# Output weights split early through DRAM, a start tile by tile, and smaller moves inside attention, in a two-layer streaming trunk

## The chip, the cores and the metric

The kernel runs on one core of a Trainium2 chip. The metric is the device time of one execution in microseconds, as the median of several runs. A core has five engines that run their own instruction queues side by side: TensorE (PE, matrix products and transposes; its weight loads are listed as PEld), VectorE (DVE), ScalarE (ACT), GpSimd (POOL) and SyncE (SP, which here issues transfers). Engines wait for each other through semaphores, and each works through its own queue in order.

## The reference

A two-layer trunk over 1024 positions of width 1024, in fp32. Each layer normalises its input, projects it once, runs three branches on slices of the projection, norms each branch, and adds the projected result:

```python
def hybrid_layer(x, positions, pre_g, w_in, ..., branch_g, w_out, post_g):
    h = rms_norm(x, pre_g)
    proj = h @ w_in
    xa, ga, q_lat, kv_lat, k_rope, gb, u, v, gc = jnp.split(proj, offsets, axis=-1)
    ya = rg_lru(causal_depthwise_conv(xa, conv_w, conv_b), wa, ba, wx, bx, lam) * jax.nn.silu(ga)
    yb = mla(q_lat, kv_lat, k_rope, positions, q_norm_g, w_uq, kv_norm_g, w_ukv) * jax.nn.silu(gb)
    yc = spatial_gating(u, v, sgu_g, sgu_bn, sgu_w, sgu_b) * jax.nn.silu(gc)
    y = jnp.concatenate([rms_norm(ya, ...), rms_norm(yb, ...), rms_norm(yc, ...)], axis=-1)
    return x + rms_norm(y @ w_out, post_g)
```

`mla` is attention with 6 heads (queries and keys of 96, values of 64) whose mask lets a position see its own chunk of 64 and all chunks before it. The branches have widths 384, 384 and 256.

## The kernel before

**Precision.** Every fp32 product is three products of a faster type (fp32r): a tensor is split into a high part, which ACT makes as a copy, and a low part, the difference, which DVE or POOL makes; `mm3` (line 124) multiplies high by high, high by low and low by high. Each weight tile and each activation that is multiplied therefore costs one ACT copy and one subtraction.

**Buffers.** Three pools of SBUF slots: `RS` (33 slots of 128x1024, for split parts), `FS` (7 fp32 slots, and rows of `Y` that are lent to it while they hold nothing) and `HS` (3 small scratch slots). `ring` holds small per-row numbers. In PSUM the banks are `pw` (two wide ones) and `pa` (four).

**Stages of a layer.** `prenorm` (line 325) squares a tile on ACT, makes the factor on POOL (`rsqrt`, line 129) and scales the tile; `turn_pair` (line 331) transposes two normed tiles and splits them. `group` (line 553) makes the inputs and gates of the recurrent branch, two column blocks at a time; then come a stage for u and v, one token tile at a time (`toks`, line 397), a stage for gc, the latent projection (`C_LAT`), the gate of attention (`C_GB`), and attention. Attention goes through 24 units of (head, pair of 128-row tiles). Each unit has `scores` (line 882: products, maximum on DVE, exponential with its sum on ACT, reciprocal on DVE, scaling on POOL) and `mixv` (line 926: transposes of the probabilities, their split, products with the values, and the gated sum of the two halves into `Y`). Scores run two units ahead of `mixv`, queries four. `project` (line 967) multiplies `Y` by `w_out` for one token tile: the first five of eight row blocks, then the last three, whose scale comes from the statistics of the attention branch (`stats`, line 510). After `project` a tile is normed, added to the input, stored, and normed again for the next layer.

**`w_out`.** From unit 8 on, whenever enough slots are free, `load_wo` (line 986) loads one of the eight row blocks of 128x1024 and splits it right there: eight ACT copies per layer and eight low parts, three of them on DVE (`WO_ON_V`), five on POOL. All transfers of the kernel are issued by SP.

**The start.** `load_pre_gain` and two tiles of x are loaded, then the first weights (`W`, line 358, in two parts of four row blocks), two more tiles, four more, and the second weights. The first two tiles are normed as a pair, so that both factors are made by one operation, then the next two, and the four others are normed by POOL.

**What sets the order.** The program order is only a wish: a scheduler places each instruction by its own timeline, and `keep` pins an instruction to its place in program order. The engine of an operation is written in the code; `Q_ON_V`, `Y_ON_V` and `WO_ON_V` are lists of the cases that go to DVE instead of POOL.

## Time and profile before

| | |
|---|---|
| median of 3 runs | 930.64 us (930.25 to 930.79) |
| the profiled execution | 928.53 us, its span 926.6 us |
| mean granted clock of PE | 0.993 |
| busy: PE, weight loads | 880.2 us (95%), 776.2 us (84%) |
| busy: DVE, ACT, POOL | 581.8 us (63%), 514.6 us (56%), 384.9 us (42%) |
| moved by transfers | 53.37 MB, 58 GB/s over the span |
| second attention loop, first attention loop | about 695 to 860 us, 245 to 400 us |

Times in the rows are microseconds from the start of the span. A group of rows comes from one of three views. The *table of stretches* cuts the span into windows; its columns are the window, its length, the busy time and number of instructions of PE, PEld, DVE, ACT and POOL, the mean granted clock of PE (1.00 is full), the busy share of the transfer engines, and GB/s. A *timeline* lists instructions in order; its columns are start, duration, engine, line, operation, output<-inputs with their shapes and types, count, and in brackets the idle time of that engine just before with the name of what ended it. The *groups by shape* sum the instructions of one line and shape; after the bar stand the busy time, the mean duration in ns, and the idle time before them. `R`, `F`, `H` are slots of the three pools.

### The profile page before, as it was taken

To read this page: it belongs to the slowest core of one execution; us is meant where nothing else is said; L and a number is where in the kernel's file an instruction comes from. 1 tells how busy PE (TensorE), PEld (TensorE's weight loads), DVE (VectorE), ACT (ScalarE), POOL (GpSimd) and SP (SyncE) were. 2 spreads that over 40 slices of the span, in tenths; PEclk is the share of its full clock that TensorE was granted. 3 is DMA by queue.
4 is the path that set the end of the run, shared out by engine and by line. 5 is a ranking of instruction groups with operands and counts; after the bars stand their busy time and mean duration, and the time that the engine had idled before them with its cause. 6 is when DMAs were issued, how large, how long until landed. Compare 5 with 4: busy or idle time off the path is not lost. (4 is left out here: it accounts for less than half of the span.)

```text
span 926.6 us, 13545 instructions
## 1 busy us (share of the span) xinstructions
PE 880.2 (95%) x5078; PEld 776.2 (84%) x5078; DVE 581.8 (63%) x1088; ACT 514.6 (56%) x1026; POOL 384.9 (42%) x407
## 2 busy tenths in 40 slices
PE   4999999999999988989999999999999998899997
PEld 3998789998898877878898888899988997788786
DVE  4568966355589988344455588354647898853422
ACT  6447634346577877344553485334567777754312
POOL 4720024152156567365743000524403566655822
PEclk9999999999999999989999999999999999999999
DMA  7201400111000211022432042000200002201322
GB/s 274 55 25 56 120 24 1 42 46 27 1 1 24 80 57 48 23 91 91 138 115 76 1 129 69 24 18 24 49 1 1 23 25 68 69 25 47 120 107 91
DMA packets 35862, 53.37 MB, mean 58 GB/s; under 512 B 7800, under 2 KB 25812, under 8 KB 35796
## 3 DMA queue, kind: packets, MB, share of 16 engines
q1 hardware_dynamic: 35796, 52.50, 17.7%
q8 instruction: 40, 0.66, 0.3%
q14 instruction: 26, 0.21, 0.1%
HBM read 44.10 MB, written 8.39 MB: 57 GB/s over the span
## 5 line engine op out<-in xcount | busy, mean ns | idle before, releaser
L125 PE MATMUL pw<-R,R 128*128 128x512 f32 (+1 forms) x704 | 259.1, 369 | 4.6 <-ACT F L916 2.3
L127 PE MATMUL pw<-R,R 128*128 128x512 f32 (+1 forms) x704 | 252.8, 360 | 0.0
L126 PE MATMUL pw<-R,R 128*128 128x512 f32 (+1 forms) x704 | 252.0, 358 | 0.0
L125 PE MATMUL pa<-R,R 128*128 128x512 f32 (+3 forms) x540 | 187.5, 349 | 2.7 <-DVE R L346 1.6
L127 PE MATMUL pa<-R,R 128*128 128x512 f32 (+3 forms) x540 | 185.9, 345 | 0.0
L126 PE MATMUL pa<-R,R 128*128 128x512 f32 (+3 forms) x540 | 185.7, 344 | 0.0
L125 PEld LDWEIGHTS pw<-R,R 128*128 128x128 f32 x704 | 134.3, 191 | 25.5 <-ACT F L916 5.0
L127 PEld LDWEIGHTS pw<-R,R 128*128 128x128 f32 x704 | 133.9, 190 | 18.5 <-POOL R L375 0.4
L126 PEld LDWEIGHTS pw<-R,R 128*128 128x128 f32 x704 | 134.3, 191 | 17.4
L125 PEld LDWEIGHTS pa<-R,R 128*128 128x128 f32 x540 | 102.0, 189 | 13.9 <-DVE R L346 2.3
L375 POOL TENSOR_TENSOR R<-F,R 128x1024 fp32r<-128x1024 f32 (+1 forms) x22 | 50.3, 2300 | 145.4 <-ACT R L374 145.3
L127 PEld LDWEIGHTS pa<-R,R 128*128 128x128 f32 x540 | 101.9, 189 | 9.9
L126 PEld LDWEIGHTS pa<-R,R 128*128 128x128 f32 x540 | 102.2, 189 | 8.4
L918 POOL TENSOR_SCALAR F<-F,ring 128x128 f32<-128x128 f32 (+3 forms) x96 | 76.3, 799 | 68.4 <-DVE ring L917 65.8
L356 DVE TENSOR_TENSOR R<-pa,R 128x512 fp32r<-128x512 f32 (+1 forms) x120 | 74.2, 628 | 21.4 <-ACT R L355 20.5
L916 ACT ACTIVATE F<-pw,ring 128x128 f32<-128x128 f32 (+3 forms) x96 | 70.9, 740 | 26.0 <-DVE ring L914 21.4
L914 DVE TENSOR_REDUCE ring<-pw 128x1 f32<-128x128 f32 (+3 forms) x96 | 71.5, 748 | 14.5 <-PE pw L907 13.8
L355 ACT ACTIVATE R<-pa 128x512 fp32r<-128x512 f32 (+1 forms) x120 | 64.3, 552 | 23.8 <-PE pa L938 18.7
L947 PE MATMUL pa<-R,R 128*128 128x256 f32 x480 | 72.5, 288 | 4.3 <-DVE H L956 2.4
L938 PE MATMUL pa<-ident,F 128*128 128x128 f32 x432 | 66.1, 276 | 10.9 <-DVE R L356 6.3
L947 PEld LDWEIGHTS pa<-R,R 128*128 128x128 f32 x480 | 63.5, 189 | 7.8 <-DVE H L956 3.7
L938 PEld LDWEIGHTS pa<-ident,F 128*128 128x128 f32 x432 | 50.4, 141 | 17.2 <-POOL Y L959 2.8
(271 smaller groups left out, 1328.0 us busy)
## 6 DMA issues: line engine op xcount, KB each, us to landing
F<-in_w_in SPq DMA_DIRECT2D x24, 512.0 KB, 4.3
F<-in_w_out SPq DMA_DIRECT2D x16, 512.0 KB, 4.0
F<-in_x SPq DMA_DIRECT2D x13, 512.0 KB, 4.5
F<-x SPq DMA_DIRECT2D x8, 512.0 KB, 4.2
x<-F SPq DMA_DIRECT2D x7, 512.0 KB
out_y<-F SPq DMA_DIRECT2D x7, 512.0 KB
...
```

Of the source, the lines that this page charges most:

```text
L125: PE.matmul(ps, lhsT=sh, rhs=mh, start=start, stop=False)
L126: PE.matmul(ps, lhsT=sh, rhs=ml, start=False, stop=False)
L127: PE.matmul(ps, lhsT=sl, rhs=mh, start=False, stop=stop)
L355: S_.activation(h, src, AF.Copy)
L356: (eng or G).tensor_tensor(out=lo, in0=src, in1=h.bitcast(F32), op=ALU.subtract)
L375: self.eng.tensor_tensor(out=lo, in0=st, in1=h.bitcast(F32), op=ALU.subtract)
L914: V.tensor_reduce(out=mx, in_=sv, axis=AX.XY, op=ALU.max, negate=True)
L916: S_.activation(p[:, 0:n].rearrange("p (a b) -> p a b", a=sv.shape[1]), sv, AF.Exp, bias=mx, accum_out=sm)
L918: G.tensor_scalar(out=p[:, 0:n], in0=p[:, 0:n], scalar1=rs, scalar2=1.0, op0=ALU.mult, op1=ALU.mult)
L938: PE.transpose(pv[:, c, i * 128:(i + 1) * 128], p[i][:, b * 128:(b + 1) * 128], ident)
L947: PE.matmul(o, lhsT=sv, rhs=pt[:, part, c * 256:(c + 1) * 256], start=(b == 0 and part == 0), stop=(b == nb - 1 and part == 1))
```

## The change

It has five parts.

1. **`w_out` is split early and kept in DRAM.** A new function `stage_wo` loads one row block, splits it into two `FS` slots and stores both parts into `wo_dram`. It is called for seven blocks in the stage of u and v and for the eighth in the stage of gc. `load_wo` no longer splits; it loads the two ready parts, with transfers that POOL issues.
2. **The start goes tile by tile.** The loads of two x tiles stand first, before the pre-norm gains and the first weights. The first three or four tiles are normed singly. The low part of the first half of the first weights is made by DVE; their second half is split inside `turn_pair`, between transposes. The first half group is walked block by block over the two outputs, the group (1, 0) of the first layer stands before the transposes of tiles 4 to 7 and takes them in between, and those tiles are normed by DVE.
3. **The gated sum.** In the 13 units of `Y_ON_V` ACT copies both halves out of PSUM and POOL adds them; DVE only multiplies by the gate. The other units are as before.
4. **Reciprocals by pairs.** The two tiles of a unit share one reciprocal.
5. **Engines of some splits.** The split of `Y` in `project` is on DVE for token tiles 2 and 3. `Q_ON_V` keeps two of its four entries, `WO_ON_V` is gone.

```diff
-Q_ON_V = ((0, 0), (0, 1), (1, 1), (4, 0))
+Q_ON_V = ((0, 0), (0, 1))
...
-WO_ON_V = (1, 4, 5)
...
+    wo_dram = [[dram.tile([128, 1024], F32, name=f"wo{k}{c}") for c in "hl"] for k in range(8)]
...
-        def split(self, order=lambda i: i):
-            for st in self.staged:
+        def split(self, order=lambda i: i, eng=None, n=8):
+            now, self.staged = self.staged[:n], self.staged[n:]
+            for st in now:
...
-                self.eng.tensor_tensor(out=lo, in0=st, in1=h.bitcast(F32), op=ALU.subtract)
+                (eng or self.eng).tensor_tensor(out=lo, in0=st, in1=h.bitcast(F32), op=ALU.subtract)
...
+    xn = [load_x(A["x"][0], t) for t in range(2)]
     load_pre_gain()
-    xn = [load_x(A["x"][0], t) for t in range(2)]
-    ws = {0: W(0, 0, 256, 4)}
+    ws = {0: W(0, 0, 256, 4, now=False)}
     xn += [load_x(A["x"][0], t) for t in range(2, 4)]
     hT = [new_hT()]
+    ws[1] = W(0, 256, 256, 4, now=False)
     x4 = [load_x(A["x"][0], t) for t in range(4, NT)]
-    ws[1] = W(0, 256, 256, 4, now=False)
     prow = load_params()
-    prenorm(xn[:2], xn[:2])
-    turn_pair(0, xn[:2], hT, 0, FS)
-    prenorm(xn[2:], xn[2:])
+    for i in range(2):
+        prenorm(xn[i:i + 1], xn[i:i + 1])
+    ws[0].split(eng=V, n=1)
+    turn_pair(0, xn[:2], hT, 0, FS, {0: lambda: ws[0].split(keep), 1: lambda: prenorm(xn[2:3], xn[2:3], keep),
+                                     3: lambda: prenorm(xn[3:4], xn[3:4], keep)})
+    ws[1].split(keep)
+    turn_pair(0, xn[2:], hT, 1, FS)
     for p in range(2):
-        prenorm(x4[2 * p:2 * p + 2], x4[2 * p:2 * p + 2], keep, G)
-    turn_pair(0, xn[2:], hT, 1, FS)
-    ws[1].split(keep)
+        prenorm(x4[2 * p:2 * p + 2], x4[2 * p:2 * p + 2], keep)
...
+            group(1, 0, lambda m: turn_pair(l, xn[2 * m:2 * m + 2], hT, 2 + m, xs, order=keep))
...
+        def stage_wo(k):
+            r = W_ROWS[k]
+            st, hi = FS.take((128, 1024)), FS.take((128, 1024))
+            h, lo = hi.bitcast(F32R), st.bitcast(F32R)
+            nc.sync.dma_start(out=st, in_=A["w_out"][l, r:r + 128, :])
+            if k < 5:
+                S_.activation(h, st, AF.Copy)
+                G.tensor_tensor(out=lo, in0=st, in1=hi, op=ALU.subtract)
+            else:
+                g = bgain(r // 128)
+                S_.activation(h, st, AF.Copy, scale=g)
+                V.scalar_tensor_tensor(out=lo, in0=st, scalar=g, in1=hi, op0=ALU.mult, op1=ALU.subtract)
+            for t, d in zip((hi, st), wo_dram[k]):
+                nc.sync.dma_start(out=d, in_=t)
+            FS.give(st)
+            FS.give(hi)
...
+            if t:
+                stage_wo(t - 1)
...
+            if t == 1:
+                stage_wo(7)
...
+            V.reciprocal(out=rs, in_=sm)
+            for i, p in enumerate(res):
+                n = (2 * j + i + 1) * 128
+                G.tensor_scalar(out=p[:, 0:n], in0=p[:, 0:n], scalar1=rs[:, i:i + 1], scalar2=1.0, op0=ALU.mult,
+                                op1=ALU.mult)
...
-            tmp = HS.take((128, 256))
-            S_.activation(tmp[mine], o[other], AF.Copy, scale=0.5)
-            V.scalar_tensor_tensor(out=tmp[mine], in0=o[mine], scalar=0.5, in1=tmp[mine],
-                                   op0=ALU.mult, op1=ALU.add)
+            tmp = HS.take((128, 2, 256))
...
+            S_.activation(tmp[mine, 0], o[other], AF.Copy, scale=0.5)
+            if on_v:
+                S_.activation(tmp[mine, 1], o[mine], AF.Copy, scale=0.5)
+                G.tensor_tensor(out=tmp[mine, 0], in0=tmp[mine, 1], in1=tmp[mine, 0], op=ALU.add)
...
-            split(Y[:, a:b, ts], yh[:, a:b], yl[:, a:b], G)
+            split(Y[:, a:b, ts], yh[:, a:b], yl[:, a:b], V if t in (2, 3) else G)
...
+            parts = RS.take((128, 1024)), RS.take((128, 1024))
+            for t, d in zip(parts, wo_dram[len(wo)]):
+                G.dma_start(out=t, in_=d)
+            wo.append(parts)
```

How instructions stand on an engine, at three places. In these pieces a number behind a name tells buffers of one pool apart: `F_134` to `F_139` are x tiles, weights or probabilities in `FS`, `R_...` split parts in `RS`, `H_...` scratch, `pa_...` and `pw_...` PSUM banks.

DVE at the start, before: both tiles are scaled (L328), then four low parts of the transposed tiles (L346), then the next two tiles.

```order
L328 TENSOR_SCALAR F_134<-F_134,ring 128x1024
L328 TENSOR_SCALAR F_135<-F_135,ring 128x1024
L346 SCALAR_TENSOR_TENSOR R_106<-pa_66,pg,R_105 128x256
L346 SCALAR_TENSOR_TENSOR R_108<-pa_67,pg,R_107 128x256
L346 SCALAR_TENSOR_TENSOR R_110<-pa_68,pg,R_109 128x256
L346 SCALAR_TENSOR_TENSOR R_112<-pa_65,pg,R_111 128x256
L328 TENSOR_SCALAR F_138<-F_138,ring 128x1024
L328 TENSOR_SCALAR F_139<-F_139,ring 128x1024
```

DVE at the start, after: the two scalings stand apart with the copy of the gains between them, and the low part of the first weights (L378) and the clearing of a gate matrix (L419) stand ahead of the low parts of the tiles.

```order
L328 TENSOR_SCALAR F_134<-F_134,ring 128x1024
L190 COPY pg<-pa_65 128x16
L328 TENSOR_SCALAR F_135<-F_135,ring 128x1024
L378 TENSOR_TENSOR R_110<-F_136,R_109 128x1024
L419 MEMSET F_136 128x768
L346 SCALAR_TENSOR_TENSOR R_102<-pa_66,pg,R_101 128x256
L346 SCALAR_TENSOR_TENSOR R_104<-pa_67,pg,R_103 128x256
L346 SCALAR_TENSOR_TENSOR R_106<-pa_68,pg,R_105 128x256
```

The subtraction at L378 has moved here from POOL.

POOL in the first layer's attention, before: splits of `w_out` (L356), scalings of probabilities (L918) and gated products (L959) take turns.

```order
L959 TENSOR_TENSOR Y<-Y,H_143 64x256
L918 TENSOR_SCALAR F_137<-F_137,ring 128x768
L942 MEMSET R_111 128x2x128
L356 TENSOR_TENSOR R_122<-F_138,R_120 128x1024
L918 TENSOR_SCALAR F_140<-F_140,ring 128x896
L959 TENSOR_TENSOR Y<-Y,H_142 64x256
L918 TENSOR_SCALAR F_136<-F_136,ring 128x1024
L356 TENSOR_TENSOR R_115<-F_139,R_114 128x1024
```

POOL at the same place, after: the loads of the ready parts (L1030, `wo1h` is the high part of block 1) stand between scalings (L954, the former L918) and gated products (L1000, the former L959).

```order
L954 TENSOR_SCALAR F_137<-F_137,ring 128x384
L954 TENSOR_SCALAR F_137<-F_137,ring 128x512
L1000 TENSOR_TENSOR Y<-Y,H_142 64x256
L1030 DMA R_110<-wo1h 128x1024
L1030 DMA R_124<-wo1l 128x1024
L1030 DMA R_120<-wo2h 128x1024
L1030 DMA R_115<-wo3l 128x1024
L1030 DMA R_114<-wo3h 128x1024
L954 TENSOR_SCALAR F_134<-F_134,ring 128x640
L954 TENSOR_SCALAR F_139<-F_139,ring 128x768
L1030 DMA R_122<-wo2l 128x1024
L1000 TENSOR_TENSOR Y<-Y,H_141 64x256
```

The splits of `w_out` are gone from this queue and 16 issues of transfers per layer have come into it, five of them in a row here.

PE at the end of the first layer's attention, before: after the last product with values (L947) four matmuls of `project` stand ahead of the statistics of the attention branch (L522).

```order
L947 MATMUL pa_68<-R_110,R_118 128x256 x4
L125 MATMUL pw_63<-R_123,R_107 128x512
L126 MATMUL pw_63<-R_101,R_107 128x512
L125 MATMUL pw_64<-R_125,R_107 128x512
L126 MATMUL pw_64<-R_126,R_107 128x512
L522 MATMUL pa_66<-ones,H_142 128x1 x4
```

PE at the same place, after: L983 is the former L947, L124 to L126 are the three products of `mm3`, and L524 is the former L522; the rows left out are matmuls of `project` too, 40 in all from the last L983 to the L524.

```order
L983 MATMUL pa_68<-R_116,R_118 128x256 x4
L983 MATMUL pa_68<-R_106,R_118 128x256 x4
L124 MATMUL pw_63<-R_123,R_103 128x512
L125 MATMUL pw_63<-R_109,R_103 128x512
L124 MATMUL pw_64<-R_125,R_103 128x512
...
L126 MATMUL pw_64<-R_112,R_108 128x512
L124 MATMUL pw_64<-R_112,R_103 128x512
L524 MATMUL pa_66<-ones,H_141 128x1 x4
L125 MATMUL pw_64<-R_133,R_103 128x512
```

So 36 more matmuls of 512 columns stand between the attention products and the statistics.

## Rows read from the trace of the kernel before

**Rows 1.** Table of stretches; columns as told under the table before.
```profile
0.00:20.00 20.00, 6.46 (x25) 5.21 (x25) 8.33 (x15) 11.83 (x21) 8.52 (x15) 1.00 0.86 314
20.00:100.00 80.00, 79.96 (x463) 70.45 (x464) 56.34 (x121) 47.20 (x72) 22.70 (x12) 1.00 0.18 52
240.00:286.00 46.00, 45.70 (x287) 41.22 (x286) 39.73 (x90) 34.48 (x86) 19.84 (x31) 1.00 0.00 1
286.00:360.00 74.00, 64.61 (x435) 57.74 (x435) 68.30 (x125) 57.77 (x123) 49.23 (x55) 1.00 0.17 58
690.00:738.00 48.00, 47.37 (x285) 41.85 (x285) 38.41 (x86) 35.64 (x84) 18.25 (x29) 1.00 0.00 1
738.00:811.00 73.00, 65.93 (x434) 58.98 (x432) 63.50 (x124) 56.92 (x123) 47.57 (x55) 0.98 0.18 58
```

**Rows 2.** Timeline of ACT at the start; columns as told under the table before.
```profile
4.33 1.06 ACT L317 ACTIVATE H<-F 128x1024 bf16<-128x1024 f32 x1 [2.33 <-DMA F<-in_x]
...
8.02 1.06 ACT L317 ACTIVATE H<-F 128x1024 bf16<-128x1024 f32 x1 [2.54 <-DMA F<-in_x]
...
9.40 1.06 ACT L374 ACTIVATE R<-F 128x1024 fp32r<-128x1024 f32 x1 [0.24 <-DMA F<-in_w_in]
...
14.85 0.47 ACT L345 ACTIVATE R<-pa,pg 128x256 fp32r<-128x256 f32 x1 [1.47 <-PE pa L339]
```

**Rows 3.** Timelines of POOL, DVE and PE at the start, and one later DVE row.
```profile
9.57 0.73 POOL L134 TENSOR_TENSOR ring<-ring,mhalf 128x2 f32<-128x2 f32 x1
10.53 5.53 POOL L375 TENSOR_TENSOR R<-F,R 128x1024 fp32r<-128x1024 f32 x2 [0.23 <-ACT R L374]
...
10.33 3.51 DVE L328 TENSOR_SCALAR F<-F,ring 128x1024 f32<-128x1024 f32 x2 [5.06 <-POOL ring L134]
...
486.30 0.75 DVE L328 TENSOR_SCALAR Y<-F,ring 128x1024 f32<-128x1024 f32 x1 [1.31 <-POOL ring L134]
...
13.90 2.82 PE L339 MATMUL pa<-ident,F 128*128 128x128 f32 x12 [1.64 <-DVE F L328]
16.38 0.78 PE L125 MATMUL pw<-R,R 128*128 128x256 f32 x2
...
32.59 0.27 PE L339 MATMUL pa<-ident,F 128*128 128x128 f32 x1
```

**Rows 4.** Table of stretches: the first transfers, and the u and v stage.
```profile
10.00:20.00 10.00, 6.02 (x24) 5.03 (x24) 7.09 (x10) 7.65 (x16) 6.78 (x5) 1.00 0.98 370
105.00:147.00 42.00, 40.95 (x191) 33.99 (x190) 27.80 (x41) 18.63 (x31) 11.15 (x9) 1.00 0.14 39
```

**Rows 5.** Groups of 286 to 360 us by shape, then one DVE timeline row.
```profile
L356 POOL TENSOR_TENSOR R<-F,R 128x1024 fp32r<-128x1024 f32 x5 | 12.0, 2392 | 1.0 <-PE pa L947 0.6 <-ACT R L355 0.3
L356 POOL TENSOR_TENSOR R<-H,R 128x512 fp32r<-128x512 f32 x6 | 8.3, 1385 | 0.0
L959 POOL TENSOR_TENSOR Y<-Y,H 64x256 f32<-64x256 f32 x5 | 4.9, 990 | 1.4 <-DVE H L956 1.3
L956 DVE SCALAR_TENSOR_TENSOR H<-pa,H 64x256 f32<-64x256 f32 x13 | 5.4, 417 | 0.8 <-ACT H L955 0.6
L917 DVE RECIPROCAL ring<-ring 128x1 f32<-128x1 f32 x27 | 3.9, 152 | 1.3 <-ACT F L916 1.3
L955 ACT ACTIVATE H<-pa 64x256 f32<-64x256 f32 x13 | 4.9, 377 | 0.3
...
293.31 2.64 DVE L959 TENSOR_TENSOR Y<-Y,H 64x256 f32<-64x256 f32 x1
```

**Rows 6.** Timeline of SP's queue: the issue of two transfers.
```profile
0.72 0.39 SPq L175 DMA_DIRECT2D F<-in_x  x1
...
26.58 1.10 SPq L256 DMA_DIRECT2D pos_i<-in_positions  x1
```

**Rows 7.** Table of stretches: between the two layers.
```profile
396.00:401.60 5.60, 2.54 (x18) 2.01 (x16) 4.69 (x5) 3.52 (x7) 5.22 (x4) 0.98 0.22 84
401.60:408.00 6.40, 6.36 (x19) 5.39 (x20) 0.79 (x2) 1.15 (x2) 6.07 (x8) 0.50 0.01 3
```

67 lines of the change are left out of this document (28 added, 39 removed).

## The prediction

> **What bounds the kernel now.** I read the page's busy row first, then the table of stretches, then who waited for whom, then the order of time where the table shows a hole. TensorE (PE) is busy 880.2 us of the 926.6 us span, so 46 us can be won from its idle time, plus what its clock loses. The table says where this lies [rows 1]: PE is busy 6.46 us of the first 20, 79.96 us of the next 80, and the attention loop shows two faces. In 240 to 286 us and 690 to 738 us, where the loop runs without the output weights, PE idles 0.3 and 0.63 us. In 286 to 360 us and 738 to 811 us, where `load_wo` brings in and splits `w_out`, it idles 74.00 - 64.61 = 9.4 us and 73.00 - 65.93 = 7.1 us, with VectorE (DVE) at 68.3 of 74. Between the two layers stands a third hole, 396 to 408 us. So there are three places: the start, the two stretches with `w_out`, and the end of the first attention.
>
> **The start.** Before, x tile 1 lands at 8.02 us [rows 2], the power that makes both factors ends at 9.57 + 0.73 = 10.30 [rows 3], and two normings take 3.51 us because GpSimd (POOL) splits the first weights in the same time (5.53 us for two). So 12 transposes start at 13.90 and matmuls at 16.38; the first group's products end where the next transposes begin, 32.59.
>
> After, tile 1 is issued right behind tile 0, pre-norm gains behind both, each tile has its own factor, and the first weight's low part is on DVE, so POOL is free then (first order piece). Unknown is when tile 1 lands: no earlier than 4.33 + 0.524 MB at 370 GB/s [rows 2, 4] = 5.8, no later than 8.0. I take the middle, 6.9. From there: 2.28 us to the factor (8.02 to 10.30), 0.75 us for one norming without POOL beside it [rows 3], 2.82 us for 12 transposes: matmuls from 12.8, 3.6 us earlier (2.5 to 4.7).
>
> Behind this ScalarE (ACT) sets the pace. From the first weight's high part, ready at 9.40 + 1.06 = 10.5, it has 16 pieces of 0.47 = 7.5 us, one more weight part (1.06), two squares (2 x 1.06, and 0.4 put on as an estimate for their read-outs: 2.5) and the two parts of the second weight (2.1): 13.2 us, to 23.7. With the last piece's DVE half and its matmuls the group ends near 25, 7.6 us earlier. I allow 1.6 us for the hop through POOL and DVE to tiles 2 and 3: **6.0 us** (2.5 to 7.6). It stays won if PE stays fed: PE was full from 20 to 100 us, and the second weight, its two POOL splits (2.8 each) and the four normings now on DVE (4 x 0.75) come well before their transposes. What is late next is the ACT queue.
>
> **Output weights leave attention.** Each layer loses, inside the loop, eight ACT copies of 128x1024 (8.5 us at 1.06), five POOL subtractions (12.0 us for five [rows 5]; four of them inside the second layer's stretch) and three DVE ones. The POOL ones cost more than themselves: DVE's product of two SBUF tiles, a small one, took 2.64 us at 293.31 while such a subtraction ran [rows 5], and PE waited. Also off DVE: one reciprocal of 0.15 us per pair (27 in this stretch, so 2.0 us), and the sum of 0.417 us in 13 of 24 units (7 of 13 here: 2.9 us). Added: ACT one more copy in those units (7 x 0.377 = 2.6 us, against 8.5 gone), POOL the sum (7 x at most 0.99 = 6.9 us) and a query split (1.4).
>
> If both stretches come down to the idle time of their neighbours, this gives 9.4 - 0.3 = 9.1 us and 7.1 - 0.6 = 6.5 us, and the second gets back the 0.02 of its clock (1.5 us): 17.1 us. Against it stand **16 transfers per layer issued by POOL**, 13 to 16 of them in these stretches, five in a row at one point (second order piece). No row shows POOL issuing a transfer. The lower bound is 0.39 us, SP's issue of a 512 KB tile [rows 6]; the upper is 2.39 us, POOL's own pass over a tile of the same form [rows 5]. I take 1.1, SP's issue of the positions [rows 6], whose pattern of single elements is the row nearest to a list made piece by piece. POOL has 74 - 49.2 + 12.0 - 6.9 - 1.4 = 28.5 us free at the old pace, some 19.5 us at the new one (65 us), for 16 issues: 1.8 and 1.2 us each. So at 1.1 it is just short of full. The five in a row hold up the next pair's normalisation by 5.5 us, which two units of lead mostly cover, not always: as an estimate I give back 3 us per layer, some half of the 5.5. **11 us** (17 down to a loss of 20, see the rivals).
>
> The Trainium skill speaks against this choice: "DMA: Bandwidth & Descriptors", section "Issuing engine by pattern", gives plain loads to SyncE, and its "Latency and other measured facts" puts about 1 us on GpSimd's making of the descriptors before the first byte. Worked out from that page, 16 us per layer would be an estimate of POOL's cost, against 17.6 by my row: the sum would come out the same within a microsecond or two. No run yet shows either.
>
> **The same work, earlier.** `stage_wo` puts into the stage of u and v 8 ACT copies (1.06 each, 8.5 us on 18.63 busy of 42), 5 POOL subtractions (12 us on 11.15), 3 on DVE, and per layer 8 loads and 16 stores of 0.524 MB, 12.6 MB. PE is full there and has eight banks to run ahead in, so engine work hides; were that cover gone, it would be up to 8.5 us per layer. The queue may not: SP issues in order, a store waits for its split, and the weights of the latent projection now stand behind stores. At 370 GB/s 12.6 MB is 34 us, on 0.14 x 42 = 6 us used now [rows 4], of 42 us: nearly full. I book 1 us per layer, **-2 us** (0 to -10).
>
> **The end of the first attention.** PE idles 5.60 - 2.54 = 3.1 us waiting for DVE's sum of squares, then runs 6.40 us at a granted clock of 0.50 [rows 7], which is 1.2 GHz, after that idle time: another 3.2 us. After, 40 matmuls of 512 columns stand behind the last attention product and ahead of these statistics, where four stood (third order piece): 36 more x 512 / 2.4 GHz = 7.7 us of work where 3.1 were missing. The splits of tiles 2 and 3 on DVE take POOL's queue out of it. **5.5 us** of 6.3 (0 to 6.3). For the last layer I book nothing.
>
> **Sum.** 6.0 + 11 - 2 + 5.5 = 20.5. The profiled execution took 928.53 us; 928.5 - 20.5 = 908.0. The median of the runs is 2.1 us above that execution, so 910.1.
>
> **The rivals.**
> - *Slower: POOL becomes the bound.* At 2.4 us per issue 16 of them are 38.4 us against 28.5 free: each stretch is 9.9 us longer than before instead of shorter, and DVE's products and ACT's copies queue behind the sums. 928.5 - 6 - 5.5 + 2 + 19.8 = 938.8, in the runs 941. It gains nothing from 1.8 us on and outweighs the other gains at about 2.1. For it: POOL is in order, and a load also waits there for its buffer's last reader. Against: SP's 0.39. Chance 0.10.
> - *POOL takes back just what the splits gave* (near 1.8 us): no gain in the two stretches, 921. Chance 0.15.
> - *Latent weights late.* If the stores fill the transfer engines, PE waits some 4 us more per layer behind u and v: 918. For it: 40 of 42 us by bandwidth; against: other matmuls are laid ahead there. Chance 0.13.
> - *The start is not carried on:* only 2.5 us of it remain, 914; inside my case. Chance 0.10.
> - *POOL issues as cheaply as SP:* 17.1 instead of 11 and no late weights, 902. Chance 0.15.
> - *The change does not do what it says:* ruled out by the order, which has all 16 loads on POOL and no split of `w_out` in attention.
>
> **How the numbers follow.** My case (904 to 916) gets 0.37, beside those above. Predicted: 910. The range reaches from 896 (the cheap issue, with the full 7.6 us of the start) to 928, which leaves out the slower rival and little else. Faster by over 0.2% (below 928.8; 0.2% is about what can be told apart here): 0.86; within: 0.03; slower: 0.11.
>
> **What would show it.** Right: first matmuls near 13 us, the transposes after the first group near 26; PE idle under 4 us in each stretch with the POOL loads; no clock of 0.50 between the layers. Wrong: rows of POOL issues above 1.2 us each, PE or DVE waiting for POOL's factors and sums; a wait of PE on ACT or POOL copies of `w_in` behind the u and v stage; tile 1 still landing at 8 us.

## The result and the profile after

The changed kernel took 943.45 us (median of 4 runs, 940.72 to 948.40), the kernel before 930.71 us in the runs beside it: a ratio of 1.0153 with a 95% interval of 1.0129 to 1.0176. It is slower by 12.7 us, where 20.5 us less were forecast. The profiled execution took 948.4 us (span 946.6), the longest of the four; before's took 928.53, so the two profiles differ by 19.9 us. Of the 7 us that this is above the difference of the medians, 5 are the profiled execution's, which ran longer than its median, and 2 are before's, which ran shorter.

The page after, engines. PE is idle 55.6 us of 946.6 where it was idle 46.4, and busy 10.8 us longer for the same 5078 matmuls, at a mean granted clock of 0.977 where it had 0.993. So of the 20.0 us between the two profiles 9.2 are longer waits and 10.8 slower running, most of it right behind waits (table of stretches):

```profile
PE 891.0 (94%) x5078; PEld 786.0 (83%) x5078; DVE 571.3 (60%) x1019; ACT 523.5 (55%) x1052; POOL 405.9 (43%) x460
```

The table of stretches after, columns as in [rows 1]:

```profile
0.00:20.00 20.00, 11.49 (x69) 9.91 (x69) 9.29 (x18) 12.91 (x21) 8.86 (x19) 1.00 0.89 316
20.00:100.00 80.00, 71.53 (x386) 62.34 (x387) 50.48 (x114) 40.16 (x64) 10.52 (x8) 0.94 0.14 37
...
37.50:45.00 7.50, 7.50 (x23) 5.98 (x24) 0.47 (x1) 0.00 (x0) 0.00 (x0) 0.67 0.00 0
150.00:159.00 9.00, 9.00 (x71) 8.56 (x69) 3.49 (x5) 3.33 (x5) 4.19 (x2) 1.00 0.96 322
159.00:166.00 7.00, 0.39 (x2) 0.34 (x2) 5.27 (x14) 1.59 (x4) 2.91 (x3) 0.71 0.88 314
...
172.00:177.00 5.00, 0.00 (x0) 0.00 (x0) 4.83 (x8) 0.90 (x1) 3.57 (x3) 0.86 0.00 0
177.00:184.00 7.00, 6.98 (x38) 6.98 (x39) 2.92 (x12) 1.55 (x3) 0.00 (x0) 0.61 0.50 149
311.00:385.00 74.00, 71.84 (x484) 65.59 (x485) 58.53 (x107) 57.59 (x135) 57.14 (x85) 1.00 0.37 122
...
417.90:424.70 6.80, 6.00 (x14) 4.73 (x15) 4.28 (x7) 1.78 (x3) 1.91 (x4) 0.50 0.42 146
757.00:836.00 79.00, 77.76 (x526) 70.72 (x525) 65.11 (x121) 63.41 (x145) 59.14 (x85) 1.00 0.32 106
```

Against [rows 1]: PE does 5.0 us more in the first 20 us, but of the next 80 it was busy 79.96 before and 71.53 now. Attention with the loads of `w_out` (311 to 385, 757 to 836) idles 2.2 and 1.2 us where it idled 9.4 and 7.1. New are two holes where `w_out` is staged, 159 to 166 and 172 to 177.

To see where the time went, the starts of the matmuls of both profiles were laid side by side at equal amounts of TensorE work (matmul columns summed from the start). How far one profile falls behind the other between two such points is that stage's loss, in us (minus: gain). The stage called staging covers u, v, gc and the latent projection; the last rows are used further down.

```
               start recur- staging gate  atten- end, next recur- staging gate atten- out   sum
                     rent   L0      L0    tion 0 layer     rent   L1      L1   tion 1
after          +7.3  +0.3   +16.4   +0.7  -9.0   +6.8      -0.0   +6.6    +3.0 -11.2  -0.9  +20.0
e1 old start   -0.2  -0.0   +11.8   +0.6  -9.0   +2.8      -0.0   +8.1    +3.1 -11.2  -0.9   +5.1
e5 group back  +4.5  -1.0    +7.8   +0.7  -9.0   +4.5      -0.0   +8.0    +3.0 -11.2  -0.9   +6.4
e2 no staging  +6.9  +0.2    -0.6   +0.7  -0.5   +1.9      -0.0   +0.0    +2.0  -4.5  -0.2   +6.1
e12 neither    +1.4  +0.4    +0.1   +1.3  -5.2   +2.9      -0.0   +0.0    +1.9  -4.8  -0.2   -2.2
e18 sums only  +1.3  +0.1    +0.3   +1.5  -4.4   +5.2      -0.0   +0.0    +2.0  -0.4  +0.8   +6.4
e15 4 blocks   +1.2  +0.0    +1.7   +1.4  -1.7   +2.1      -0.0   +4.8    +3.5  -3.9  -0.5   +8.6
e8 4 in gate   -0.5  -0.0    +1.5  +10.7  -7.2   -2.8      -0.0   +5.2    +9.3  -4.9  -0.2  +11.2
e10 in groups  +3.8  +2.4    +2.8   +2.6  -9.0   +3.7      -0.1   +3.6    +0.8  -6.0  -0.4   +4.2
```

Attention gives back 20.2 us, more than forecast. The start, the staging and the end of the first attention each lose what they should have gained or left alone. Each row is of one profile: by the same reckoning e3, whose start is that of the changed kernel, loses 5.1 us there and not 7.3, so differences of a microsecond or two between rows are not to be read.

### The profile page after: what moved, and what is told of

It is laid out like the page before. It is cut to its first block, busy times and chain, and to the rows that moved or that the text cites. A ratio compares the mean times of both kernels' runs of the same rounds, so it can differ in the third digit from the quotient of the medians.

```text
span 946.6 us, 13689 instructions
## 1 busy us (share of the span) xinstructions
PE 891.0 (94%) x5078; PEld 786.0 (83%) x5078; DVE 571.3 (60%) x1019; ACT 523.5 (55%) x1052; POOL 405.9 (43%) x460
## 4 chain that ended last, share of the span: by engine, by line
PE 71%; DVE 11%; ACT 7%; DMA 4%; issue 4%; POOL 2%; SPq 1%; DVEq 0%; POOLq 0%; ACTq 0%
PE pw L124 12%; PE pw L125 12%; PE pw L126 12%; PE pa L124 7%; PE pa L126 7%; PE pa L125 7%; PE pa L983 5%; PE pa L974 4%; DMA F<-in_w_in 1%; DMA F<-in_w_out 1%; DVE R L358 1%; PE pw L939 1%; DVE R L378 1%; ACT F L948 1%; PE pa L339 1%
## 5 line engine op out<-in xcount | busy, mean ns | idle before, releaser
L124 PE MATMUL pw<-R,R 128*128 128x512 f32 (+1 forms) x704 | 262.6, 375 | 19.9 <-DVE Y L441 7.0
L126 PE MATMUL pw<-R,R 128*128 128x512 f32 (+1 forms) x704 | 256.1, 365 | 4.4 <-DVE R L358 4.4
L125 PE MATMUL pw<-R,R 128*128 128x512 f32 (+1 forms) x704 | 256.4, 365 | 0.2 <-DVE R L346 0.2
L124 PE MATMUL pa<-R,R 128*128 128x512 f32 (+3 forms) x540 | 187.8, 349 | 11.5 <-DVE F L716 10.1
L126 PE MATMUL pa<-R,R 128*128 128x512 f32 (+3 forms) x540 | 185.6, 346 | 0.0
L124 PEld LDWEIGHTS pw<-R,R 128*128 128x128 f32 x704 | 137.0, 196 | 42.5 <-issue 7.2
L126 PEld LDWEIGHTS pw<-R,R 128*128 128x128 f32 x704 | 137.1, 195 | 23.9 <-DVE R L358 4.8
L125 PEld LDWEIGHTS pw<-R,R 128*128 128x128 f32 x704 | 137.9, 196 | 18.8 <-DVE R L346 0.8
L124 PEld LDWEIGHTS pa<-R,R 128*128 128x128 f32 x540 | 102.2, 189 | 22.6 <-DVE F L716 10.7
L126 PEld LDWEIGHTS pa<-R,R 128*128 128x128 f32 x540 | 102.2, 189 | 9.9
L954 POOL TENSOR_SCALAR F<-F,ring 128x128 f32<-128x128 f32 (+3 forms) x96 | 71.3, 755 | 37.5 <-DVE ring L951 33.7
L378 POOL TENSOR_TENSOR R<-F,R 128x1024 fp32r<-128x1024 f32 (+1 forms) x21 | 49.6, 2368 | 74.2 <-ACT R L377 74.2
L983 PE MATMUL pa<-R,R 128*128 128x256 f32 x480 | 75.8, 290 | 2.4 <-DVE R L358 2.0
L983 PEld LDWEIGHTS pa<-R,R 128*128 128x128 f32 x480 | 64.7, 189 | 6.6 <-DVE R L358 2.6
L1116 POOL TENSOR_TENSOR F<-F,F 128x1024 f32<-128x1024 f32 (+2 forms) x20 | 40.2, 2011 | 51.0 <-DVE F L1023 50.8
```

Source lines behind the costliest of these rows:

```text
L124: PE.matmul(ps, lhsT=sh, rhs=mh, start=start, stop=False)
L125: PE.matmul(ps, lhsT=sh, rhs=ml, start=False, stop=False)
L126: PE.matmul(ps, lhsT=sl, rhs=mh, start=False, stop=stop)
L378: (eng or self.eng).tensor_tensor(out=lo, in0=st, in1=h.bitcast(F32), op=ALU.subtract)
L954: G.tensor_scalar(out=p[:, 0:n], in0=p[:, 0:n], scalar1=rs[:, i:i + 1], scalar2=1.0, op0=ALU.mult, op1=ALU.mult)
L983: PE.matmul(o, lhsT=sv, rhs=pt[:, part, c * 256:(c + 1) * 256], start=(b == 0 and part == 0), stop=(b == nb - 1 and part == 1))
```

## Experiments

Ratios are to the kernel before in the same series, with 95% intervals. Except where said, an experiment is the changed kernel with the edit shown.

### Which part costs

**e1: the old start**, all else as changed.

```diff
-    xn = [load_x(A["x"][0], t) for t in range(2)]
     load_pre_gain()
+    xn = [load_x(A["x"][0], t) for t in range(2)]
...
+        for p in range(2):
+            turn_pair(l, xn[2 * p:2 * p + 2], hT, 2 + p, xs)
```

> The changed kernel with the start of the old one: loads, normings by pairs, first weights, and group (1, 0) behind the transposes of tiles 4 to 7, all as before. By my reading of the two traces (time at equal TensorE work) the new start costs 7.3 us, in one stall of 7.0 us and the low clock behind it. Then this kernel is 7 us faster than the changed one, near 936, and the stall near 30 us is gone. Rival: the lost time is swallowed later, because the stalls behind u and v come from transfers that keep their own pace; then it stays at 941 to 944.

Measured: 933.67 us, 1.0059 (1.0034 to 1.0083), 9.8 us below the changed kernel. The new start costs; it does not help. By the table its cost is not in the start alone: staging and the end of the first attention shrink too (11.8 for 16.4, 2.8 for 6.8). In the staging the order on the engines comes out different. At the end of the attention PE's waits are nearly the same (4.4, 1.8 and 2.6 us for 4.4, 1.8 and 2.9); what differs is the clock behind the short ones (last section).

**e2: no staging**, `load_wo` as before, the new start kept.

```diff
-            if t:
-                stage_wo(t - 1)
...
+            eng = V if k in WO_ON_V else G
+            if k < 5:
+                split(st, h, lo, eng)
```

> The changed kernel with the old handling of the output weights: no staging, loads on SP and splits inside attention; the new start, the gated sums, the pairwise reciprocals and the splits in project stay. Theory: staging costs 22 to 23 us (17 in the first layer, 5 to 6 in the second), and taking the splits out of attention gave most of the 19 to 20 us that the two attentions gained; then this kernel is within 5 us of the changed one, 938 to 948. Rival: the sums and reciprocals alone gave the gain in attention; then it is some 20 us faster than the changed one, near 922.

Measured: 933.97 us, 1.0048 (1.0028 to 1.0067), 9.5 us below the changed kernel, between the two cases named. The staging loses more than attention wins by it, although it does win there (second attention -4.5 without, -11.2 with).

**e12: neither**, that is, the kernel before with gated sums, paired reciprocals, and the moved splits of queries and `project`.

```diff
-Q_ON_V = ((0, 0), (0, 1), (1, 1), (4, 0))
+Q_ON_V = ((0, 0), (0, 1))
...
-            split(Y[:, a:b, ts], yh[:, a:b], yl[:, a:b], G)
+            split(Y[:, a:b, ts], yh[:, a:b], yl[:, a:b], V if t in (2, 3) else G)
```

> The kernel before with the small parts of the change alone: gated sums on ScalarE and GpSimd in 13 units, reciprocals by pairs, two query splits back on GpSimd, and the splits of tiles 2 and 3 in project on VectorE. No staging, the old start. From the two undone parts I expect their difference: 934.0 of the kernel without staging, minus 7 for the start, 925 to 929, that is 1 to 4 us faster than before. If these parts need the freed engines of the other part, it is no faster, 929 to 932.

Measured: 928.06 us, 0.9987 (0.9963 to 1.0011): no difference that can be told. By the table the small parts alone gain 5.2 and 4.8 us in the two attentions. In e2, which has them too, with the new start, the same columns gain only 0.5 and 4.5.

**e18: gated sums and paired reciprocals only**, against before.

```diff
+            V.reciprocal(out=rs, in_=sm)
...
+                G.tensor_tensor(out=tmp[mine, 0], in0=tmp[mine, 1], in1=tmp[mine, 0], op=ALU.add)
```

> The kernel before with the gated sums and the reciprocals by pairs alone; staging, start, the query splits and the splits in project are as before. The run with all small parts lost 2.9 us at the end of the first attention and ended level. If that loss belongs to the splits on VectorE, this kernel keeps the 2 to 4 us gained in attention: 924 to 927. If it belongs to the order that the scheduler chooses there anyway, 927 to 930.

Measured: 931.56 us, 1.0034 (1.0018 to 1.0050), longer than either case named. Against e12 it is 3.5 us longer, so the moved splits are worth about that in a kernel without staging. The profiled execution of e18 lies 3.6 us above its median and that of e12 1.8 below, so the table does not tell where. `project` waits 5.9 us on POOL here and 4.4 on DVE in e12.

**e3: `project`'s splits back on POOL**, in the changed kernel.

```diff
-            split(Y[:, a:b, ts], yh[:, a:b], yl[:, a:b], V if t in (2, 3) else G)
+            split(Y[:, a:b, ts], yh[:, a:b], yl[:, a:b], G)
```

> The changed kernel with the splits of tiles 2 and 3 in project back on GpSimd. Theory: the stall of 4.4 us and the low clock behind it at the end of the first attention (some 7 us) come from VectorE, whose four splits take 5.17 us there beside GpSimd's work; then this kernel is 3 to 7 us faster, 936 to 940. Rival: GpSimd's queue is as late, as in the kernel before; then the stall stays in another place and the time is 942 to 945.

Measured: 945.63 us, 1.0179 (1.0155 to 1.0202), 2.2 us above the changed kernel with intervals that overlap: no cause of the loss. `project` waits 5.9 us on POOL here, as in e18, where the changed kernel waits 4.4 on DVE.

### The start

After, the timelines of ACT, DVE, POOL and PE at the start:

```profile
5.86 1.06 ACT L317 ACTIVATE H<-F 128x1024 bf16<-128x1024 f32 x1
...
18.55 2.83 DVE L328 TENSOR_SCALAR F<-F,ring 128x1024 f32<-128x1024 f32 x1 [0.77 <-POOL ring L133]
...
28.99 1.42 DVE L328 TENSOR_SCALAR Y<-Y,ring 128x1024 f32<-128x1024 f32 x2 [2.60 <-POOL ring L133]
31.33 1.41 DVE L328 TENSOR_SCALAR Y<-Y,ring 128x1024 f32<-128x1024 f32 x2 [0.93 <-POOL ring L133]
32.67 0.23 DVE L215 COPY par<-pa 128x80 f32<-128x80 f32 x1
...
34.60 3.36 DVE L441 SCALAR_TENSOR_TENSOR Y<-pw,par,Y 128x511 f32<-128x511 f32 x5
...
18.48 2.35 POOL L378 TENSOR_TENSOR R<-F,R 128x1024 fp32r<-128x1024 f32 x1
...
11.54 0.58 PE L124 MATMUL pw<-R,R 128*128 128x256 f32 x2
...
21.44 2.36 PE L339 MATMUL pa<-ident,F 128*128 128x128 f32 x12 [2.26 <-DVE F L328]
...
37.46 0.77 PE L124 MATMUL pw<-R,R 128*128 128x512 f32 x1 [7.03 <-DVE Y L441]
```

Tile 1 lands by 5.86 us and products start at 11.54. At equal work the kernel is 7.2 us ahead of before's 25 us, but only 2.3 us ahead of its 30 us. What it loses there begins at the norming of tile 3 on DVE: it takes 2.83 us beside POOL's split of the second weights, where [rows 3] have 0.75 for one alone. PE waits 2.26 us for it and then runs at a granted clock of 0.50 from 22.0 to 25.4.

Then group (1, 0) finds the PSUM banks of the first group full. They are freed by the convolution (L441), which needs the parameters. Their copy (L215) stands on DVE behind four normings, and these wait for their factors. PE stands still for 7.03 us, and then runs 7.5 us at a granted clock of 0.67 (table above), 7.5 x 0.33 = 2.5 us more.

**e9: the parameters ahead of the four normings.**

```diff
-    for p in range(2):
-        prenorm(x4[2 * p:2 * p + 2], x4[2 * p:2 * p + 2], keep)
     turn_params(prow)
+    for p in range(2):
+        prenorm(x4[2 * p:2 * p + 2], x4[2 * p:2 * p + 2], keep)
```

> The changed kernel with the transposed parameters copied out ahead of the normings of tiles 4 to 7. In the changed kernel the copy of the parameters stands on VectorE behind four normings, which wait for four squares on ScalarE: it runs at 32.67 us though its transpose was done at 25.6, and the convolutions that free the first group's PSUM start at 33.9. Theory: this is what the stall of 7.0 us waits for; with the copy at 26 us the stall shrinks below 3 us and the kernel is 4 to 8 us faster than the changed one, 935 to 939. Rival: the convolutions wait for VectorE's normings in any order; then the stall stays above 5 us, 941 to 945.

Measured: 940.19 us, 1.0112 (1.0091 to 1.0132); 3.3 us less by the medians, with intervals that just overlap. The same wait is shorter by 2.1 us, less than expected. The 4.9 us that stay are the convolution itself, which nothing covers: ACT's copy and DVE's steps of 0.74 us, with two of the normings still between them. Waits of PE in the first 50 us of e9 (total, times, longest):

```profile
PE pw L124 <- DVE Y L441: 4.9, 1, 4.9
```

**e5: group (1, 0) back behind the transposes** of tiles 4 to 7.

```diff
-            group(1, 0, lambda m: turn_pair(l, xn[2 * m:2 * m + 2], hT, 2 + m, xs, order=keep))
+        for p in range(2):
+            turn_pair(l, xn[2 * p:2 * p + 2], hT, 2 + p, xs)
```

> The changed kernel with only one piece of the new start undone: group (1, 0) stands again behind the transposes of tiles 4 to 7, not ahead of them. Theory: the new start is right up to 30 us (the first group ends 2.4 us earlier), and the stall of 7 us comes from the interleaving alone, because group (1, 0) needs PSUM that the convolutions of the first group free late, behind four squares and four normings of 1.0 and 0.7 us each; with the transposes in between the stall is under 2 us and the kernel is 6 to 9 us faster than the changed one, 934 to 938. Rival: the transposes wait as long, since they need the same four normed tiles; then the stall stays at 5 us or more, and the time within 3 us of 943.

Measured: 935.42 us, 1.0070 (1.0046 to 1.0094), 8.0 us won. The wait for L441 is gone. But the two profiles, 13.6 us apart (20.0 - 6.4), differ by 2.8 in the start, 1.3 in the recurrent stage and 8.6 in the staging, where the scheduler's order changed with the move. The start still is 4.5 us behind before. Waits of PE in the first 50 us of e5 (L339 are the transposes), and its table of stretches:

```profile
PE pa L339 <- DVE R L346: 2.8, 2, 2.5
```
```profile
28.00:36.00 8.00, 4.32 (x31) 3.52 (x30) 7.07 (x18) 4.87 (x11) 1.22 (x2) 0.85 0.32 78
36.00:45.00 9.00, 8.67 (x36) 7.05 (x36) 5.54 (x12) 3.58 (x8) 0.00 (x0) 0.76 0.00 1
```

With the group back in its place, PE waits for DVE, which now has the four normings and is busy 7.07 of 8 us; PE idles 3.7 us and then runs at 0.76 for 9 us (9.0 x 0.24 = 2.2 us). So the start is lost in more than one place: by the moved group, and by what DVE makes there now. That the 4.5 us are the normings' is read from this trace; no run has the new start with the normings on POOL.

### The staging

The chain of waits after, 133 to 178 us: start, length, who had the chain. L623 and L624 are ACT's copy and POOL's low part in `stage_wo`, `wo4l<-F` is the store of such a part, L275 to L277 steps of the rope tables on DVE, L716 the product on gc that frees a PSUM bank; "issue" is time for which the profile shows no cause.

```profile
133.15 3.69 DMA F<-in_w_out
136.92 1.07 ACT Y L623
138.07 2.40 POOL F L624
...
141.47 4.43 issue
...
151.81 2.39 POOL F L624
154.21 5.97 DMA wo4l<-F
...
170.47 1.94 DVE Y L275
172.44 1.60 DVE Y L276
...
176.63 0.34 DVE F L716
177.02 0.58 PE pw L124
```

PE's missing work runs through the blocks of `w_out`: load, copy, low part, store, and then the slot that the store frees, for which DVE stands with the first step of the rope tables (L299 below). By the table of stretches the transfer engines are busy 0.96 of 150 to 159 us and not at all in 172 to 177: they are full in bursts, not over the stage. ACT's waits, after (118 to 172 us) first, then before (111 to 165):

```profile
ACT Y L623 <- DMA F<-in_w_out: 7.6, 2, 5.8
ACT Y L623 <- issue: 7.1, 1, 7.1
```
```profile
ACT F L657 <- PE pa L127: 11.5, 4, 4.8
```

Before, ACT waits for PE; after, it waits for `w_out`. Up to 159 us this costs PE nothing. The two holes are waits for L716 (PE's waits of 100 to 205 us), and the rows at the first one show what L716 stands behind: ACT's copy of a latent weight (L377) with the tanh of gc (L715) right after it, and DVE's clearing (L299), with which the rope tables begin. The last row is ACT in the second layer:

```profile
PE pa L124 <- DVE F L716: 6.6, 1, 6.6
PE pw L124 <- DVE F L716: 6.1, 2, 5.3
```
```profile
161.14 0.79 ACT L377 ACTIVATE R<-Y 128x704 fp32r<-128x704 f32 x1 [3.32 <-DMA Y<-in_w_in]
161.84 0.64 ACT L715 ACTIVATE H<-pa 128x256 f32<-128x256 f32 x2
...
160.42 0.48 DVE L299 MEMSET F<- 128x512 f32 x1 [1.91 <-DMA wo4l<-F]
...
631.33 0.79 ACT L377 ACTIVATE R<-F 128x704 fp32r<-128x704 f32 x1 [4.52 <-DMA F<-in_w_in]
```

At the first hole two things come late together: a latent weight, issued at 154.63 us among the stores, and the slot of a store. At the second, DVE makes steps of the rope tables in 2.01, 1.59 and 1.59 us ahead of L716. The second layer has no rope tables; there ACT waits 4.52 us for a latent weight, and PE 3.48 us for the L716 behind it. The experiments that follow ask which link counts.

**e7: no stores.** It leaves out the 16 stores per layer; `load_wo` loads `w_out` itself in place of both parts.

```diff
-            for t, d in zip((hi, st), wo_dram[k]):
-                nc.sync.dma_start(out=d, in_=t)
```

> Leaves out the 16 stores per layer; the ready parts are read from w_out itself, so the result is not the reference's. The loads, the eight copies and the eight subtractions of the staging stay where they are, as do the 16 loads in attention. Theory: what hurts behind u and v is the transfer queue, full with 8.4 MB of stores per layer that the latent weights queue behind, and the slots that a store holds; then 12 to 20 us of the 23 come back, 923 to 931. Rival: the engines' own staging work (copies, subtractions that slow VectorE down) is the cause; then the time stays at 938 or above.

Measured: 940.83 us, 1.0121 (1.0083 to 1.0160); staging 11.1 and 9.5 us, 20.6 together where the changed kernel has 23.0. The stores alone are not the cause.

**e11: only transfers.** It leaves out the copies and subtractions of `stage_wo`; the loaded block is stored twice in place of its two parts.

```diff
-                S_.activation(h, st, AF.Copy)
-                G.tensor_tensor(out=lo, in0=st, in1=hi, op=ALU.subtract)
...
-            for t, d in zip((hi, st), wo_dram[k]):
+            for t, d in zip((st, st), wo_dram[k]):
```

> Leaves out the staging's eight copies and eight subtractions per layer; the loaded block is stored twice as it is, so the result is not the reference's. Its 24 transfers per layer and its slots stay. If ScalarE's copies that wait for the staged blocks in the order of its queue are the cause, 10 to 17 us of the 23 come back, 926 to 934. If it is the transfers and slots alone (late weights of the latent projection, the rope table's slot), at most 8 us come back, 935 to 943.

Measured: 941.73 us, 1.0119 (1.0086 to 1.0153); staging 6.9 and 4.8 us. So half of the 23.0 us is there with transfers and slots alone, and half goes with the engine work. The kernel is only 1.7 us faster by the medians, because in this order the attentions gain some 12 us and not 20. What is left is the rival of late latent weights: ACT's waits in e11, 118 to 170 us, both for such a weight:

```profile
ACT R L377 <- DMA Y<-in_w_in: 14.0, 2, 7.7
```

**e4 and e6: the latent weights' copies behind gc**, in e4 by program order, in e6 pinned there.

```diff
-        w, wl = wgc, W(l, C_LAT, 352, 2)
+        w, wl = wgc, W(l, C_LAT, 352, 2, now=False)
...
+        wl.split(keep)
```

> The changed kernel with the split of the latent weights placed behind the loop over gc instead of ahead of it, so that ScalarE's and GpSimd's queues hold no copy that waits for those loads in front of the tanh of gc. Theory: the two stalls of 6.6 and 5.3 us at 159 and 172 us and the 3.5 us at 629 are TensorE waiting for PSUM banks that ScalarE and VectorE could not free because their queues stood behind late weights; then 10 to 20 us of 23 come back, 923 to 933. Rival: the transfers themselves are too late for the latent projection; then the stall moves behind gc and the time stays within 5 us of 943.

> The run before this one of the same idea left ScalarE's order unchanged and so tested nothing. Here the copies of the latent weights are pinned behind the first layer's and second layer's loop over gc, so that eight tanh of gc stand ahead of them on ScalarE. Theory: copies that wait for late loads hold the tanh, and with them TensorE's banks; then the first stall near 159 us and the one near 629 us go, 6 to 14 us come back, 930 to 937. Rival: the latent weights are needed right behind; then the wait moves to the first products of the latent projection, and the time is 938 to 946.

Measured: e4 945.71 us, 1.0176 (1.0145 to 1.0206), but ACT's queue came out in the same order as without the edit, so it told nothing. e6 959.14 us, 1.0322 (1.0282 to 1.0362): staging 20.5 and 14.7 us. With these copies out of the way of gc PE's waits for L716 shrink (6.8 us for 12.7, first layer), as the theory has it, but 5.1 us of waits for the copies and low parts of the latent weights come in behind, as the rival has it, and the whole is 15.7 us longer than the changed kernel. Where the rest of that comes from was not followed.

**e17: the latent weights loaded ahead of the staging.**

```diff
+        wl = W(l, C_LAT, 352, 2, now=False)
         wgc = W(l, C_GC, 256, 4)
...
-        w, wl = wgc, W(l, C_LAT, 352, 2)
+        w = wgc
+        wl.split()
```

> The changed kernel with the four loads of the latent weights issued ahead of the staging's loads and stores; they keep four of the seven to nine free slots until gc begins, which leaves three for the staging. Theory after the run with the rope tables moved: the cost in the first layer is mainly copies of late latent weights (and what follows them on ScalarE, GpSimd and VectorE); then the first layer's cost falls from 17 to under 8 us and the kernel to 928 to 936. Rival: the staging itself, with its copies that wait for loads and slots on ScalarE, holds the gelu and tanh; with fewer slots that gets worse: 940 or more.

Measured: 970.23 us, 1.0455 (1.0441 to 1.0468), the worst of all: staging 25.6 us. The latent weights were there and copied with waits of at most 0.6 us; but three of their four pieces held slots until they were copied at 152 to 155 us. One wait of PE and what is behind it, in e17: PE's wait, ACT's waits (L627 is the copy of the later blocks) and the DVE row that ACT's copy let go:

```profile
PE pa L124 <- DVE F L718: 20.2, 1, 20.2
```
```profile
ACT Y L623 <- DMA F<-in_w_out: 12.2, 2, 6.9
...
ACT Y L627 <- DMA wo4l<-Y: 4.8, 1, 4.8
```
```profile
184.43 1.28 DVE L628 SCALAR_TENSOR_TENSOR F<-F,par,Y 128x1024 fp32r<-128x1024 f32 x1 [12.83 <-ACT Y L627]
```

DVE stands 12.83 us behind a copy of `w_out`, whose slot waits for stores. So late weights are not needed for a loss: with early weights and fewer slots the staging itself holds L716. It does not show that late weights cost the changed kernel nothing; the rows above have them in both layers. Slots that go round through DRAM, in queues that PE's own work shares, are what e11, e17 and the rows have in common. How the 23.0 us divide between late weights, slots and engine work, beyond the halves of e11, is not shown.

**e13 and e16: rope tables before the staging**, e16 on top of e15 below.

```diff
+        if l == 0:
+            rope_tables()
         wgc = W(l, C_GC, 256, 4)
```

> The changed kernel with the rope tables of the first layer made ahead of the stage of u and v, not between it and gc. Open is why staging costs 17 us in the first layer and 5 to 6 in the second. Theory: the difference is the rope tables, which only the first layer has: some 25 small operations of VectorE, the first of which waits for a slot that a store still reads, the others stretched from 0.23 to 1.6 or 2.0 us each beside GpSimd's late splits, all ahead of the products that free TensorE's banks. Then the first layer's loss falls to 5 to 8 us and the kernel is 8 to 12 us faster than the changed one, 931 to 936. Rival: late weights alone; then 940 to 945.

> The run with four staged blocks, with the rope tables ahead of the stage of u and v too. With so little staging the tables have few late splits beside them; I expect a change of at most 2 us against that run, to the better.

Measured: e13 964.39 us, 1.0374 (1.0347 to 1.0401); e16 953.59 us, 1.0256 (1.0237 to 1.0276). Both expectations failed. In the chain the tables stand last, ahead of L716, but taking them out of there makes it worse by 21 and 17 us, and in e13 PE still waits 7.1 us for L716. So moving them is no cure, and the loss does not need them, as the second layer shows. Why the early tables cost so much was not settled.

**e8, e10, e14, e15: fewer blocks per stage**, all with the old start. e15 stages four blocks, one per two tiles of u and v, and splits the other four in attention as before. e8 puts the other four into the stage of the gate, e14 behind half groups of the recurrent branch. e10 has all eight behind half groups.

```diff
-            if t:
-                stage_wo(t - 1)
+            if t % 2:
+                stage_wo(t // 2)
```
```diff
+        stage = lambda i: lambda m: stage_wo(i + m)
+        group(0, 1, stage(0))
+        group(1, 1, stage(2))
```

> The changed kernel with the old start, four blocks staged (in the stage of u and v, at every second token tile) and the other four loaded and split inside attention as before. If the gain in attention goes with the number of splits that leave it, half of 20 us is left, against 6 us for the staging and 3 between the layers: 926 to 930. If the first four take most of the gain, since the stalls stand in the middle of the attention, 918 to 924.

> The changed kernel with the old start, and with the staging spread: four row blocks in the stage of u and v (every second token tile) and four in the stage of the attention gate, none in the stage of gc. If the loss is one of transfers crowded into 42 us, half of them there leave the latent weights in time; then it is 12 to 18 us faster than the changed kernel with the old start (933.7), 915 to 922, and faster than the kernel before. If each staged block costs its own engine work wherever it stands, it is 928 to 936.

> The changed kernel with the old start, and with four blocks staged behind the half groups (0, 1) and (1, 1) and four in the stage of u and v, at every second token tile. From the run with four blocks there (cost 1.9 us in the first layer, 4.6 in the second) and the run with eight behind the half groups (some 5 and 3.3 us) I expect a cost of 6 to 12 us, against 20 us gained in the attentions and 3 lost between the layers: 919 to 926. If the costs don't go down with the number of blocks, 930 to 935.

> The changed kernel with the old start, and with the eight blocks staged in the stage before: one behind each half group of (0, 1), (1, 1), (2, 0) and (2, 1), where GpSimd has 60 us without work. Theory: staging hurts only where copies that wait for its transfers stand ahead of the engine work that frees PSUM for TensorE, and where the next weights need its slots; there the convolutions free few banks and the 12 us behind u and v are spared: 12 to 18 us faster than the changed kernel with the old start (933.7), 915 to 922. Rival: the next weights, those of u and v, are late instead, and the stall only moves to the start of that stage: 930 to 940.

Measured: e15 936.61 us, 1.0070 (1.0050 to 1.0090); e8 942.47, 1.0147 (1.0103 to 1.0191); e14 939.02, 1.0099 (1.0077 to 1.0120); e10 934.70, 1.0057 (1.0032 to 1.0083). Eight blocks in the stages of u, v and gc cost 11.8 us in the first layer (e1), four cost 1.7 (e15). The first layer's price grows far faster than the work, as a stage with few free slots would make it, which is argued and not shown; in the second the step is smaller (8.1 and 4.8). No place took the other four for nothing: 10.7 us in the gate's stage (e8), 2.4 and 2.8 in the groups (e10), where the scheduler's new order also moved the start by 3.8. And e15 gains only 1.7 and 3.9 us in the attentions with half of the splits out of them, less than e12 with all of them in. Of the four, e10 fell into its rival's range; the three others took longer than any case named for them.

None of these versions beats the kernel before; e12 is level with it.

## Why the prediction was wrong, step by step

**The start: 6.0 us won were forecast, 7.3 were lost.** The first steps held: tile 1 by 5.86 us (forecast 6.9), products from 11.54 (12.8), and 7.2 us won at before's 25 us. Three steps failed behind that.

- "1.6 us for the hop through POOL and DVE to tiles 2 and 3" was 4.9: the price of 0.75 us for a norming holds "without POOL beside it", and POOL's split of the second weights ran beside this one.
- "It stays won if PE stays fed" priced the transposes of tiles 4 to 7 and named the ACT queue as the next late thing. But the diff also moved group (1, 0) ahead of these transposes, which had covered the time in which the convolution empties PSUM. PE stands still for 7.03 us. Of these 2.1 are the parameters behind the normings (e9), the others the convolution. e5 undoes the move and has 2.8 of the 7.3 us back in the start, 8.0 in the whole.
- The four normings "come well before their transposes", 3 us booked as hidden. They come just ahead of them, and in e5 PE waits there for DVE. That the 4.5 us left in e5 are theirs is read from the trace alone.

**`w_out` out of attention: 11 us forecast, 20.2 in the table.** The mechanism held and its main price was too high. POOL's timeline after, the first two of the five issues in a row:

```profile
336.51 0.59 POOL L1030 DMA_DIRECT2D R<-wo1h  x1 [1.36 <-PE pa L983]
337.10 0.54 POOL L1030 DMA_DIRECT2D R<-wo1l  x1
```

An issue takes 0.53 to 0.78 us, not the 1.1 of [rows 6], and the five in a row hold POOL for 2.8 us instead of 5.5, so the 3 us per layer given back were not due. Both stretches came to 2.2 and 1.2 us of idle time, near the 0.3 and 0.6 aimed at. With the column of the gate, which ends inside the attention loop, the table has 16.5 us won, close to the 17.1 that the prediction had before it gave back 6. The Trainium skill, "DMA: Bandwidth & Descriptors", section "Latency and other measured facts", puts about 1 us before the first byte of such a transfer; as the time that POOL's queue is held, for which the prediction's estimate beside the sum took it, it is too much by these rows. But the gain is not the staging's alone: sums, reciprocals and moved splits without staging have 10.0 us in e12 and 5.0 in e2. The prediction booked both in one term, so the runs test only their sum; that it came out so near is in part luck, since e15 and e11 gain far less with the same sums and reciprocals.

**The staging: 2 us booked, 23.0 lost** (16.4 and 6.6). The step that failed is "PE is full there and has eight banks to run ahead in, so engine work hides", and with it the 1 us per layer for "The queue may not". Both looked at sums: 8.5 us of ACT, 12 of POOL, 34 of transfers in 42 us. Every sum fits. The order does not: each block has to come in before ACT may go on, the latent weights stand among the stores, and what lets PE's banks go (tanh on ACT, L716 on DVE) stands behind late weights, slots and steps that POOL slows down. Without the engine work 11.7 of the 23.0 us are left (e11), so it did not hide; what is left is the queue and the slots, 5.9 us per layer for the 1 booked. The rival of late latent weights, priced at 4 us a layer, is in the rows of both layers and in e11; e17 shows that early weights, bought with slots, are no cure. How large the loss comes out depends on the order too: with the same eight blocks in the first layer it is 16.4 us here, 11.8 in e1 and 7.8 in e5; which placements make that difference was not pinned down. DVE's small steps are drawn out besides: a step of 128x128 takes 0.23 us before and 1.59 after, beside a POOL subtraction. DVE before, DVE after, POOL after:

```profile
147.20 0.23 DVE L276 TENSOR_SCALAR Y<-Y 128x128 f32<-128x128 f32 x1
```
```profile
172.44 1.59 DVE L276 TENSOR_SCALAR Y<-Y 128x128 f32<-128x128 f32 x1
```
```profile
172.28 1.66 POOL L378 TENSOR_TENSOR R<-F,R 128x704 fp32r<-128x704 f32 x1
```

The prediction saw this in attention [rows 5] and did not carry it over to where the POOL work went. The Trainium skill, "SBUF — State Buffer", section "SBUF: two separate sides", says that DVE, in some of its modes, and GpSimd lock a pair of ports for a whole instruction, so the later one waits it out; the rows agree, since the DVE step ends 0.09 us after POOL's.

**The end of the first attention: 5.5 us won were forecast, 6.8 were lost**, the first group of the next layer included. The 36 matmuls do stand ahead of the statistics, and the wait of [rows 7] is gone. The step that failed is "The splits of tiles 2 and 3 on DVE take POOL's queue out of it". Timelines of DVE, POOL and PE:

```profile
413.95 5.17 DVE L358 TENSOR_TENSOR R<-Y,R 128x640 fp32r<-128x640 f32 x4
...
413.43 2.80 POOL L1116 TENSOR_TENSOR F<-F,F 128x1024 f32<-128x1024 f32 x1
...
418.70 0.79 PE L126 MATMUL pw<-R,R 128*128 128x512 f32 x1 [4.39 <-DVE R L358]
...
447.20 0.50 PE L124 MATMUL pw<-R,R 128*128 128x512 f32 x1 [1.77 <-ACT F L1021]
...
512.79 0.47 PE L124 MATMUL pw<-R,R 128*128 128x512 f32 x1 [2.85 <-DVE F L441]
```

The wait came back behind the 36 matmuls: `project` waits 4.39 us for the splits of tiles 2 and 3, and DVE, which begins them at 413.95, takes 5.17 us beside POOL's work. The clock is 0.50 from 417.9 to 424.7, as long as before, against the sign "no clock of 0.50 between the layers". At equal work this stretch is 0.5 us longer than before's, so it only failed to gain. Most of the 6.8 us was lost behind it: in a wait of 1.77 us for ACT's copy out of PSUM in `project` (L1021) and one of 2.85 us for the convolution of the next layer, each with a low clock behind (0.65 from 447.2 to 452.1, 0.59 from 512.8 to 517.0). With POOL as the splitter the first wait is 5.9 us and the one for L1021 0.7 (e18, e3), so it is not shown that the move to DVE helped here.

**The rivals.** "POOL becomes the bound" gave 941, close to 943, but by another mechanism: POOL's issues are cheap, and attention is faster. "Latent weights late" had the right stage at a third of the size, and "The start is not carried on" kept 2.5 us of a start that lost 7.3; no rival had a loss of this size in these places. The lower end of the range, 896, is not what its terms give either: cheap issue and the full start come to 902 - 1.6 = 900.

The parts don't add: without the new start the kernel is 9.8 us faster, without the staging 9.5, without both 15.4 (943.45 - 928.06). Where one part goes, the scheduler's order for the others changes too.
